# Layer 0's middle in a written order of TensorE, VectorE and ScalarE, and late modulation columns computed by TensorE

## Chip, cores and metric

The kernel runs on one core of one Trainium2 chip. Times are device microseconds (us) of one launch. Names: PE is TensorE, DVE VectorE, ACT ScalarE, POOL GpSimd, SP the engine that issues the DMAs spoken of here. The TensorE clock that the profile shows as granted is 1.00 at 2.4 GHz and 0.50 at 1.2 GHz; shares between are means over a stretch.

## What is computed

Two decoder layers on 1024 tokens of width 1024, in f32. Layer 0 has the even mixer, layer 1 the attention. The change concerns the even mixer and the modulation of both layers:

```python
def even_mixer(h, w_in, dw_w, dw_b, ln_w, ln_b, lam_re, lam_im, log_dt,
               b_re, b_im, c_re, c_im, d_skip, glu_w, glu_b, w_out):
    proj = h @ w_in
    a_in = proj[..., :2 * CONV_WIDTH]
    a_z = proj[..., 2 * CONV_WIDTH:3 * CONV_WIDTH]
    u = proj[..., 3 * CONV_WIDTH:3 * CONV_WIDTH + SSM_WIDTH]
    b_z = proj[..., 3 * CONV_WIDTH + SSM_WIDTH:]
    ya = conformer_conv(a_in, dw_w, dw_b, ln_w, ln_b) * jax.nn.silu(a_z)
    ys = jax.nn.gelu(s5_ssm(u, lam_re, lam_im, log_dt, b_re, b_im, c_re, c_im, d_skip), approximate=False)
    ys = ys * jax.nn.sigmoid(ys @ glu_w + glu_b)
    ys = ys * jax.nn.silu(b_z)
    return jnp.concatenate([ya, ys], axis=-1) @ w_out
```

`conformer_conv` is a gate, a causal depthwise convolution of 31 taps, a layer norm over channels and a SiLU; `s5_ssm` a diagonal complex recurrence. Each layer has 24 modulation columns of 128 numbers (8 shifts, 8 scales, 8 gates): the conditioning vector c times `mod_w`, plus `mod_b`.

## The kernel before

**Products.** Every large f32 product is done as three fp32r matmuls (`mm3`, L225 to L227): each operand is split into a rounded part and a rest (`split`, L203 on ScalarE and L206 on VectorE: `wh`, `wl` for weights, `h0h`, `h0l` for the hidden state). A projection of 128 output channels (`proj`) is two halves of 512 tokens (`pj`), each 8 blocks x 3 = 24 matmuls of 128x128 by 128x512. The GLU (`pg`) has 4 blocks, 12 matmuls a half; the output projection (`po`) comes last.

**State-space part.** `ssm_quarter(j)` does a quarter of the channels. Its head builds angles on VectorE (`T`, `TS`, L1387 to L1390) and sines on ScalarE (L1391 to L1393), powers on GpSimd (`HC`, L1402 to L1408), a small product `pk` on PE (L1417: eight matmuls of 128x32 by 128x128 in four column groups, by `tile_position`), a trip through DRAM (`Kd` to `M`, eight DMAs), and, with GpSimd's `G` and `GS` (L1438 to L1443), transposes `pgt`, products `sr`, `si`, the recurrence (`V`, `W`, scans L1469, `X`) and `py`. `TS`, `HT`, `G` and `GS` share a ring of three buffers (tag `t2`):

```python
n = L(f"TS{j}", "t2", [128, 4, 128], 3)
tt = L(f"HT{j}", "t2", sh, 3)
tg = L(f"GS{j}", "t2", sh, 3)
```

**Convolution.** `conv(j)` writes its gated input to DRAM and back (`Uc`), builds weight matrices `cm` on VectorE (L674), and multiplies (`pc`, L679, 64x64 tiles).

**Late modulation.** Sixteen columns of layer 0 are ready before the projections. The other 32 (8 gates of layer 0 and all of layer 1) come from `mod_cols`: two 256 KB DMAs a column (L253) into one buffer `mw` of two halves, two multiply-and-sum instructions on VectorE (L232) and an add (L255).

**Order.** A scheduler orders every engine's queue by priority: the program text gives the rank, and `prio` shifts it (`mod_cols` and the rope tables with 400000, which puts them behind other work that is ready by its reckoning). Each engine then runs its queue strictly in that order; a waiting instruction holds up all behind it on its engine.

Of the kernel before, what the change touches and what calls it, by code (L numbers as in the profile page):

```python
# [9 lines left out]
F32 = mybir.dt.float32  # L10
# [53 lines left out]

class Trunk:
# [30 lines left out]
    def prep(self):  # L96
# [22 lines left out]
        self.mod = [[self.consts.tile([128, 1], F32, name=f"mod{i}_{m}") for m in range(24)] for i in range(2)]  # L119
# [15 lines left out]
        self.g = [[self.consts.tile([128, 1], F32, name=f"g{i}_{m}") for m in range(8)] for i in range(2)]  # L135
# [99 lines left out]
    def mod_scale(self, layer, m):  # L235
        if 8 <= m < 16:
            nw = _cols()["norm_w"][0] + layer * 8 + m - 8
            self.nc.vector.scalar_tensor_tensor(self.g[layer][m - 8], self.mod[layer][m], 1.0, self.pk[:, nw:nw + 1],
                                                ALU.add, ALU.mult)

    def mod_bias(self, layer, m):
        o = _cols()["mod_b"][0] + layer * 24 + m
        return self.pk[:, o:o + 1]

    def mod_cols(self, cols):

        nc = self.nc
        w = self.u("mw", tag="mw")
        for layer, m in cols:
            h = self.c0.tile([128, 2], F32, tag="mh", name="mh", bufs=2)  # L250
            for i in range(2):
                c = slice(512 * i, 512 * i + 512)
                nc.sync.dma_start(w[:, c], self.I["mod_w"][layer, m][:, c])  # L253
                self.dot_c(h[:, i:i + 1], w[:, c], c)
            nc.vector.scalar_tensor_tensor(self.mod[layer][m], h[:, 0:1], h[:, 1:2], self.mod_bias(layer, m),  # L255
                                           ALU.add, ALU.add)
            self.mod_scale(layer, m)


    def layer0(self):  # L260
        nc, tc, I = self.nc, self.tc, self.I
        with self.cx0 as cx:
# [48 lines left out]
            with tc.tile_pool(name="start", bufs=8) as sp, order:  # L311
# [46 lines left out]
                def mods(m):  # L358
                    c = self.mod[0][m]
                    self.dot_c(c, mw[m], slice(0, 1024))  # L360
                    nc.vector.tensor_tensor(c, c, self.mod_bias(0, m), op=ALU.add)
                    self.mod_scale(0, m)
# [52 lines left out]
                pu, place = self.ssm_u_psum(ps, pm)  # L415
# [37 lines left out]
            self.ssm_params()  # L453

            def proj(j, evac):
                if j not in wt:
                    load_w(j, I["w0"][j], 8)
                hi, lo = wt.pop(j)
                for h in range(2):
                    p = ps(f"pj{j}_{h}")  # L460
                    s = slice(h * 512, (h + 1) * 512)
                    for k in range(8):
                        self.mm3(p, hi[:, k], lo[:, k], hh[k][:, s], hl[k][:, s], k == 0, k == 7)
                    evac(h, p)
# [4 lines left out]
            ysg = [None] * 4  # L469
            us = [self.ssm_u(j, pu) for j in range(3)]  # L470
            last = {}
            proj(15, lambda h, p: last.update({(3, h): p}))
            us.append(self.ssm_u(3, last))
            for j in range(4):
                self.ssm_quarter(j, us[j], pm, ysg)

            cut = lambda a, b: a.rearrange("p (t c) -> p t c", t=8)[:, :, b * 64:b * 64 + 64]
            late = lambda a: a.rearrange("p (c t) -> p t c", t=8)
            short = lambda a: a.rearrange("p (t c) -> p t c", t=8)
            acc = []  # L480
            for j in range(4):
                sg = [None, None]
                at = S(f"at{j}", tag="cv")

                def ev_gate(h, p):
                    sg[h] = E(f"sg{j}_{h}")
                    nc.scalar.activation(short(sg[h]), late(p), AF.Sigmoid)

                def ev_a(h, p):
                    nc.vector.tensor_tensor(cut(at, h), late(p), short(sg[h]), op=ALU.mult)  # L490

                proj(4 + j, ev_gate)
                proj(j, ev_a)
                acc.append(self.conv(j, at, pc))

            def ev_bz(h, p):
                t = E("z")
                nc.scalar.activation(short(t), late(p), AF.Silu)
                nc.sync.dma_start(self.bzd[j][:, h * 512:(h + 1) * 512], t)

            for j in range(4):
                proj(16 + j, ev_bz)

            with self.prio(400000):
                self.mod_cols([(0, m) for m in range(16, 24)] + [(1, m) for m in range(24)])
                self.rope_tables()


            sx.close()
            ga = cx.enter_context(tc.tile_pool(name="gluA", bufs=4))  # L510
            gx = cx.enter_context(ExitStack())
            gb = gx.enter_context(tc.tile_pool(name="gluB", bufs=4))
            zp = gx.enter_context(tc.tile_pool(name="z", bufs=4))
            Z = lambda: zp.tile([128, 512], F32, tag="z", name="z")
            ysh, ysl = [], []
            for j in range(4):
# [4 lines left out]
            for m in range(4):  # L521
                load_w(f"g{m}", I["glu_w"][m], 4)
                hi, lo = wt.pop(f"g{m}")
                for h in range(2):
                    p = ps(f"pg{m}_{h}")
                    s = slice(h * 512, (h + 1) * 512)
                    for k in range(4):
                        self.mm3(p, hi[:, k], lo[:, k], ysh[k][:, s], ysl[k][:, s], k == 0, k == 3)
                    t = E(f"gs{m}_{h}")
                    nc.scalar.activation(t, p, AF.Sigmoid, bias=self.P["glu_b"][:, m:m + 1])  # L530
                    nc.vector.tensor_tensor(ysg[m][:, s], ysg[m][:, s], t, op=ALU.mult)
# [10 lines left out]
            for j in range(4):  # L542
                for b in range(2):
                    yc[4 + j][b] = (gb, ga)[b].tile([128, 2, 512], F32R, tag="g", name=f"yc{4 + j}_{b}")
                    z = Z()
                    nc.sync.dma_start(z, self.bzd[j][:, b * 512:b * 512 + 512])
                    y = cut(ysg[j], b)
                    nc.vector.tensor_tensor(y, y, short(z), op=ALU.mult)
                    split_y(4 + j, ysg[j], b)


            for b in range(2):
                mu = pm(f"mu{b}")
# [1054 lines left out]
```

## Time and profile before

| | us |
|---|---|
| three runs: median (lowest to highest) | 1705.69 (1701.48 to 1708.97) |
| the profiled execution | 1709.29 |
| its span (first to last instruction) | 1707.5 |
| PE busy in it | 1654.8 (97%) |
| DVE busy | 1009.0 (59%) |
| ACT busy | 610.2 (36%) |
| POOL busy | 521.2 (31%) |
| layer 0's middle: first `pj` of layer 0 to first `pj` of layer 1 | 72.87 to 500.30 |

The profiled execution is 1.8 us longer than its span, and 3.6 us over the median of the runs. "Busy" counts the time in which an engine had an instruction running; for PE it counts the same at either clock.

### The profile page before, as it was taken

The numbers are of one execution on the slowest core, as the hardware profiler recorded it, in microseconds if no ns is written. First come the engines' busy times: TensorE is split into PE (matmuls) and PEld (weight loads), VectorE is DVE, ScalarE is ACT, GpSimd is POOL, SyncE is SP. The second block draws the span as 40 slices with busy tenths as digits, with TensorE's granted clock in tenths as the row PEclk, the third lists the DMA queues.
The fourth block names the chain that finished last, engine by engine and source line by source line (L and its number), as shares of the span: only waits on it lengthen the run. The fifth ranks groups of instructions, "written<-read, shape, count | busy, mean of one in ns | idle before, by whom it ended". The sixth has DMA issues, their size and how long they took to land.

```text
span 1707.5 us, 27738 instructions
## 1 busy us (share of the span) xinstructions
PE 1654.8 (97%) x9992; PEld 1516.7 (89%) x9992; DVE 1009.0 (59%) x2489; ACT 610.2 (36%) x1847; POOL 521.2 (31%) x737
## 2 busy tenths in 40 slices
PE   8989797999999999999999999999999999999999
PEld 5767576878789999999999999999999999999887
DVE  8987766175667545645754754754564575565541
ACT  5423231274534333333333334333333333343410
POOL 6466200100145323332431431432333233334000
PEclk9989898999999999999999999999999999999999
DMA  9366666313542112112212211211310211111252
GB/s 352 110 193 176 188 196 189 117 63 128 193 146 58 31 38 83 47 29 63 69 35 60 82 35 49 80 38 39 83 53 21 76 59 38 48 62 63 87 175 91
DMA packets 94186, 159.78 MB, mean 94 GB/s; under 512 B 13281, under 2 KB 43745, under 8 KB 94050
## 3 DMA queue, kind: packets, MB, share of 16 engines
q1 hardware_dynamic: 94050, 158.02, 30.2%
q8 instruction: 79, 1.29, 0.3%
q14 instruction: 57, 0.47, 0.1%
HBM read 130.54 MB, written 23.23 MB: 90 GB/s over the span
## 4 chain that ended last, share of the span: by engine, by line
PE 80%; DVE 1%; ACT 1%; POOL 0%; issue 0%; DMA 0%; DVEq 0%; ACTq 0%; POOLq 0%
PE pj L225 19%; PE pj L227 19%; PE pj L226 19%; PE O L985 4%; PE S L936 4%; PE po L227 3%; PE po L225 3%; PE po L226 3%; PE tqk L890 2%; PE tP L963 2%; DVE x L211 1%; PE pg L226 0%; PE pg L225 0%; PE pg L227 0%; PE pc L679 0%; DVE x L820 0%
## 5 line engine op out<-in xcount | busy, mean ns | idle before, releaser
L225 PE MATMUL pj<-wh,h 128*128 128x384 f32 x1536 | 544.0, 354 | 0.0
L227 PE MATMUL pj<-wh,h 128*128 128x384 f32 x1536 | 517.7, 337 | 0.8 <-DVE h L218 0.8
L226 PE MATMUL pj<-wl,h 128*128 128x384 f32 x1536 | 516.4, 336 | 0.0
L226 PEld LDWEIGHTS pj<-wl,h 128*128 128x128 f32 x1536 | 290.3, 189 | 0.3 <-issue 0.2
L225 PEld LDWEIGHTS pj<-wh,h 128*128 128x128 f32 x1536 | 289.6, 189 | 1.1 <-issue 0.2
L227 PEld LDWEIGHTS pj<-wh,h 128*128 128x128 f32 x1536 | 289.0, 188 | 1.4 <-DVE h L218 1.4
L875 POOL TENSOR_TENSOR B<-u,sin 128x256 f32<-128x256 f32 x192 | 190.3, 991 | 207.4 <-DVE u L871 207.4
L847 ACT ACTIVATE sq<-pj 128x128 f32<-128x128 f32 x384 | 103.0, 274 | 353.1 <-PE pj L227 327.5
L848 POOL TENSOR_SCALAR ss<-ss 128x2 f32<-128x2 f32 x192 | 41.2, 215 | 501.4 <-ACT sq L847 501.2
L206 DVE TENSOR_TENSOR wl<-raw,wh 128x768 fp32r<-128x768 f32 (+1 forms) x124 | 115.9, 949 | 123.9 <-ACT wh L203 123.3
L912 DVE COPY qk<-tqk 128x256 f32<-128x256 f32 x188 | 79.1, 421 | 139.6 <-PE tqk L890 139.6
L871 DVE SCALAR_TENSOR_TENSOR u<-pj,ss,pk 128x128 f32<-128x128 f32 x384 | 116.3, 344 | 75.7 <-POOL ss L849 75.7
L849 POOL TENSOR_TENSOR ss<-ss,mh 128x2 f32<-128x2 f32 x192 | 140.5, 732 | 16.0
L956 ACT ACTIVATE E<-E,nm 128x256 f32<-128x256 f32 (+2 forms) x128 | 71.3, 557 | 198.2 <-DVE nm L955 198.2
L226 PE MATMUL pj<-h0l,wh 128*128 128x512 f32 x272 | 110.2, 405 | 0.0
L227 PE MATMUL pj<-h0h,wl 128*128 128x512 f32 x272 | 109.1, 401 | 0.6 <-DVE wl L206 0.6
L225 PE MATMUL pj<-h0h,wh 128*128 128x512 f32 x272 | 109.6, 403 | 0.0
L883 DVE TENSOR_TENSOR u<-A,B 128x128 f32<-128x128 f32 x192 | 56.1, 292 | 88.0 <-POOL B L875 81.6
L203 ACT ACTIVATE wh<-raw 128x768 fp32r<-128x768 f32 (+1 forms) x124 | 97.5, 792 | 29.2 <-PE po L226 15.2
L882 DVE TENSOR_TENSOR A<-u,cos 128x256 f32<-128x256 f32 x192 | 96.6, 503 | 4.4
L936 PE MATMUL S<-qk 128*128 128x128 f32 x544 | 86.4, 274 | 0.0
L232 DVE CUSTOM_DVE_ANT_0 mw<-mw,cb 128x512 f32<-128x512 f32 (+1 forms) x72 | 61.5, 862 | 40.4 <-DMA mw<-in_mod_w 40.1
(429 smaller groups left out, 2858.1 us busy)
## 6 DMA issues: line engine op xcount, KB each, us to landing
raw<-in_wqkv SPq DMA_DIRECT2D x92, 384.0 KB
mw<-in_mod_w SPq DMA_DIRECT2D x64, 256.0 KB
wr<-in_w SPq DMA_DIRECT2D x17, 512.0 KB
al<-ad SPq DMA_DIRECT2D x16, 512.0 KB
wro<-in_wo SPq DMA_DIRECT2D x11, 512.0 KB
x<-in_x SPq DMA_DIRECT2D x8, 512.0 KB
mw<-in_mod_w SPq DMA_DIRECT2D x8, 512.0 KB
mw<-in_shift SPq DMA_DIRECT2D x8, 512.0 KB
```

The costliest lines, as they stand in the source:

```text
L203: nc.scalar.activation(hi, src, AF.Copy)
L206: getattr(nc, leng).tensor_tensor(lo, src, hi.bitcast(F32), op=ALU.subtract)
L225: mm(ps, lhsT=lh, rhs=rh, start=first, stop=False)
L226: mm(ps, lhsT=lh, rhs=rl, start=False, stop=False)
L227: mm(ps, lhsT=ll, rhs=rh, start=False, stop=last)
L847: sc.activation(sq[:, i], p[:, i * 128:(i + 1) * 128], AF.Square, accum_out=ss[:, i:i + 1])
L849: gp.tensor_tensor(ss, ss, mh, op=ALU.pow)
L871: v.scalar_tensor_tensor(u[:, i].rearrange("p a b -> p (a b)"), p[:, i * 128:(i + 1) * 128], ss[:, i:i + 1], w, ALU.mult, ALU.mult)
L875: gp.tensor_tensor(f(B), f(u), sin[:, ti].unsqueeze(1).to_broadcast([128, 4, 64]), op=ALU.mult)
L882: v.tensor_tensor(f(A), f(u), cos[:, ti].unsqueeze(1).to_broadcast([128, 4, 64]), op=ALU.mult)
L912: v.tensor_copy(out, tp)
L936: pe.matmul(ps[:, i * 128:(i + 1) * 128], lhsT=qT[h, g, t], rhs=kT[h, g, kt], start=True, stop=True)
```

## The change

From the first projection of layer 0 to the start of layer 1, the order of PE, DVE and ACT is that of the program text (`manual_schedule`); POOL and SP are ordered by the scheduler as before. The text is a loop over slots: 42 slots t of one half each (key 15, then 4, 0, 5, 1, 6, 2, 7, 3, then 16 to 19, g0 to g3, 8 to 11), then 21 slots of the output projection. A slot evacuates the half before it (`evac`), splits the next key's weights (`begin`), runs the side jobs that a table `side` gives for that slot, does a step of the modulation, and then issues its own 24 (or 12) matmuls. `ssm_quarter` and `conv` become generators that stop at each `yield`; step s of quarter j stands at slot 4j + (2, 3, 5, 6, 7, 7, 8, 11). The rope tables come at slot 1, layer norm at slots 25 to 34. PSUM: ring `ps` keeps 3 banks, `pm` goes from 3 to 2, and one bank `pr` is new.

`mod_cols` goes. `mod_rows` makes eight groups of four columns: in each of four steps two 256 KB DMAs bring weights with the input on partitions, and eight f32 matmuls (c repeated in 32 columns, by 128x128) run in four column groups; ACT copies the rows out, and `mod_turn` turns them into columns with one matmul `mc` of four columns and one add on DVE. The bytes fetched are the same.

```diff
-    def mod_cols(self, cols):
-        nc = self.nc
-        w = self.u("mw", tag="mw")
-        for layer, m in cols:
-            h = self.c0.tile([128, 2], F32, tag="mh", name="mh", bufs=2)
-            for i in range(2):
-                c = slice(512 * i, 512 * i + 512)
-                nc.sync.dma_start(w[:, c], self.I["mod_w"][layer, m][:, c])
-                self.dot_c(h[:, i:i + 1], w[:, c], c)
-            nc.vector.scalar_tensor_tensor(self.mod[layer][m], h[:, 0:1], h[:, 1:2], self.mod_bias(layer, m),
-                                           ALU.add, ALU.add)
...
+    def mod_rows(self, ps, pr):
...
+        w = self.u("mw", tag="mw").rearrange("p (i m n) -> p i m n", i=2, m=4)
+        crep = self.cb[:, 0:256].rearrange("p (k n) -> p k n", k=8)
+        rows = self.cb[:, 256:384]
+        p = pr("pr")[:, 0:128]
+        for n, (layer, m) in enumerate(MODR):
+            for q in range(4):
+                for i in range(2):
+                    nc.sync.dma_start(w[:, i], self.I["mod_r"][n, 2 * q + i])
+                yield
+                for i in range(2):
+                    k = 2 * q + i
+                    for j in range(4):
+                        nc.tensor.matmul(p[32 * j:32 * j + 32], lhsT=crep[:, k], rhs=w[:, i, j], start=(k == 0),
+                                         stop=(k == 7), tile_position=(0, 32 * j))
+            nc.scalar.activation(rows, p, AF.Copy)
+            self.mod_late = (ps, rows, layer, m)
...
+        c = ps(f"mc{layer}{m}")[:, 0:4]
+        nc.tensor.matmul(c, lhsT=rows, rhs=self.ident[:, 0::32], start=True, stop=True)
...
+            cx.enter_context(tc.manual_schedule(engines={mybir.EngineType.DVE, mybir.EngineType.Activation,
+                                                         mybir.EngineType.PE}))
...
+            seq = [15]
+            for j in range(4):
+                seq += [4 + j, j]
+            seq += [16, 17, 18, 19, "g0", "g1", "g2", "g3", 8, 9, 10, 11]
+            seq += [f"o{m}b" for m in range(5)] + [f"o{m}a" for m in range(5)]
+            seq += [f"o{m}" for m in range(5, 8)] + [f"p{m}" for m in range(8)]
...
+            def begin(i):
+
+                if i + 1 < len(seq) and seq[i + 1] not in wt:
+                    split_w(seq[i + 1])
...
+            at(1, self.rope_tables)
             for j in range(4):
...
+                for t in (2, 3, 5, 6, 7, 7, 8, 11):
+                    at(4 * j + t, next, quarter[j], None)
+                for t in (8, 9, 10, 12):
+                    at(4 * j + t, lambda j: next(conv[j], None), j)
...
+            for b in range(2):
+                at(25, ln_sum, b)
+                t = 27 + 4 * b
+                at(t, ln_mean, b)
+                at(t, ln_center, b, 0)
+                at(t + 1, ln_center, b, 1)
+                at(t + 2, ln_var, b)
+                at(t + 2, ln_rsqrt, b)
+                at(t + 3, ln_norm, b, (0, 1, 2, 3))
...
+            for t in range(42):
+                i, h = divmod(t, 2)
+                key = seq[i]
+                if done:
+                    evac(*done)
+                if h == 0:
+                    begin(i)
+                for fn in side.pop(t, ()):
+                    fn()
+                self.mod_turn()
+                if 4 <= t < 26 or t in (27, 31) or t > 33:
+                    mod_step()
+                p = ps(f"p{key}_{h}")
...
+                for k in range(n):
+                    self.mm3(p, hi[:, k], lo[:, k], rh[k][:, s], rl[k][:, s], k == 0, k == n - 1)
+                done = (key, h, p)
...
+            for k in range(8):
+                at(57 + k // 2, hidden, k)
...
         for t in range(8):
             nc.sync.dma_start(M[t::8], kd[:, :, (7 - t) * 16:(7 - t) * 16 + 128])
+        yield
```

**PE at the first quarter's `pk`.** Before, in the second projection (`pj_1_870` is its first key's second half, `pj_0_1486` the next key's first half, `pk_922` the quarter's product):

```order
L226 MATMUL pj_1_870<-h0l_753,wh_778 128x512
L227 MATMUL pj_1_870<-h0h_752,wl_779 128x512
L1417 MATMUL pk_922<-HC_909,bbd_820 32x128
L1447 MATMUL pgt_953<-ident,G_944 128x128 x4
L225 MATMUL pj_0_1486<-h0h_442,wh_782 128x512
L226 MATMUL pj_0_1486<-h0l_443,wh_782 128x512
L227 MATMUL pj_0_1486<-h0h_442,wl_783 128x512
L225 MATMUL pj_0_1486<-h0h_512,wh_782 128x512
L226 MATMUL pj_0_1486<-h0l_513,wh_782 128x512
L227 MATMUL pj_0_1486<-h0h_512,wl_783 128x512
L225 MATMUL pj_0_1486<-h0h_553,wh_782 128x512
L1417 MATMUL pk_922<-HC_909,bbd_820 32x128 x7
```

After (`p_1_857` is the half of slot 1, `p_0_936` that of slot 2):

```order
L232 MATMUL p_1_857<-h0l_714,wh_739 128x512
L233 MATMUL p_1_857<-h0h_713,wl_740 128x512
L1575 MATMUL pk_915<-HC_902,bbd_781 32x128 x8
L231 MATMUL p_0_936<-h0h_403,wh_743 128x512
L232 MATMUL p_0_936<-h0l_404,wh_743 128x512
L233 MATMUL p_0_936<-h0h_403,wl_744 128x512
```

One `pk` matmul, the transposes and seven large matmuls stood ahead of the other seven `pk`; now all eight stand ahead of slot 2's large matmuls.

**POOL for the same quarter, after the change** (the same six operations in the same order stand in the queue before it; `HC_902` is what `pk_915` reads, and `Activation` is ACT's semaphore):

```order
L1598 TENSOR_TENSOR GS_966<-bbi,pir 128x512 [waits DVE_49,Activation_49]
L1564 TENSOR_TENSOR HT_903<-pk,pr 128x512 [waits Pool_49]
L1599 TENSOR_TENSOR G_964<-G_964,GS_966 128x512 [waits Pool_49]
L1565 TENSOR_TENSOR HC_902<-HC_902,HT_903 128x512 [waits Pool_49]
L1601 TENSOR_TENSOR GS_966<-bbi,prr 128x512 [waits Pool_49]
L1566 TENSOR_SCALAR HC_902<-HC_902 128x512 [waits Pool_49]
```

What moved is not this queue but the angle `T` and its sines on DVE and ACT, whose buffer `TS` the first row takes over.

**DVE at the first angles.** Before (`T_901` is quarter 0, `T_1047` quarter 1; `h0l` belongs to the work ahead of the projections):

```order
L1387 TENSOR_TENSOR T_901<-pk,t_304 128x512
L1387 TENSOR_TENSOR T_1047<-pk,t_304 128x512
L218 SCALAR_TENSOR_TENSOR h0l_753<-x_332,mod_7_86,h0h_752 128x512
L1389 TENSOR_SCALAR TS_902<-T_901 128x512
L218 SCALAR_TENSOR_TENSOR h0l_753<-x_332,mod_7_86,h0h_752 128x512
L206 TENSOR_TENSOR wl_779<-wr_373,wh_778 128x1024
L1390 SCALAR_TENSOR_TENSOR TS_902<-TS_902,T_901 128x512
L206 TENSOR_TENSOR wl_783<-wr_375,wh_782 128x1024
```

After (`wl_889` is the split for key 0, in slot 2's `begin`; `ro` ends the rope tables of slot 1):

```order
L177 TENSOR_SCALAR ro<-ro 128x512
L182 SCALAR_TENSOR_TENSOR ro<-ro 128x512
L183 TENSOR_SCALAR ro<-ro 128x512
L212 TENSOR_TENSOR wl_889<-wr_338,wh_888 128x1024
L1545 TENSOR_TENSOR T_894<-pk,t_265 128x512
L1547 TENSOR_SCALAR TS_895<-T_894 128x512
L1548 SCALAR_TENSOR_TENSOR TS_895<-TS_895,T_894 128x512
L1579 COPY kp_779<-pk_915 128x128
```

Quarter 0's angle stood among the last hidden-state rests, quarter 1's beside it; now quarter 0's stands in slot 2 behind the split, and quarter 1's in slot 6.

**ACT in the layer norm's two halves.** Before (`lq` squares, `lr` the root, `cv` the SiLU of the normed convolution, `z` the gate of a projection):

```order
L186 ACT_TABLE_LOAD
L186 ACTIVATE lr_3102<-va_3085,eps 128x512
L188 ACTIVATE lr0t<-lr_3102 128x512
L564 ACTIVATE lq_3126<-cv_1697 128x512
L567 ACTIVATE lq_3129<-cv_1920 128x512
L579 ACT_TABLE_LOAD
L579 ACTIVATE z<-pj_0_3225 128x512
L564 ACTIVATE lq_3134<-cv_2143 128x512
L567 ACTIVATE lq_3137<-cv_2366 128x512
L574 ACTIVATE cv_1697<-cv_1697,pk 128x8x64
```

After (`gs` is the GLU's sigmoid, `whg` its weights):

```order
L683 ACTIVATE gs_0_2970<-pg_0_2957,pk 128x512
L192 ACT_TABLE_LOAD
L192 ACTIVATE lr_2976<-va_2973,eps 128x512
L194 ACTIVATE lr0t<-lr_2976 128x512
L683 ACT_TABLE_LOAD
L683 ACTIVATE gs_1_2997<-pg_1_2984,pk 128x512
L209 ACTIVATE whg_3000<-wrg_2791 128x512
L607 ACT_TABLE_LOAD
L607 ACTIVATE cv_1532<-cv_1532,pk 128x8x64
L607 ACTIVATE cv_1946<-cv_1946,pk 128x8x64
L607 ACTIVATE cv_2361<-cv_2361,pk 128x8x64
L607 ACTIVATE cv_2700<-cv_2700,pk 128x8x64
```

The layer norm stood among the projections 8 to 11, whose gates are SiLU too; now it stands among the GLU halves, with a table load at each change of function.

## Rows read from the trace of the kernel before

**Rows 1.** Busy time by engine over layer 0's middle, with PE's granted clock.

```profile
core 0: us, PE busy (x) PEld busy (x) DVE busy (x) ACT busy (x) POOL busy (x), PEclk, DMA share, GB/s
72.87:500.30 427.43, 389.03 (x2368) 309.06 (x2366) 280.21 (x480) 155.75 (x227) 108.26 (x81) 0.93 0.53 164
```

**Rows 2.** PE's waits in that stretch, by what ended them (total, times, longest).

```profile
PE pc L679 <- DVE cm L674: 8.3, 3, 4.6
PE py L1491 <- DVE X L1479: 7.3, 3, 4.0
PE pc L679 <- DMA Uc<-Cd: 5.8, 2, 3.5
PE py L1487 <- DMA mw<-in_mod_w: 5.8, 1, 5.8
PE po L227 <- DVE wlo L206: 5.2, 1, 5.2
```

**Rows 3.** Timeline of PE: start, duration; 44 matmuls between the two rows' starts.

```profile
319.67 0.39 PE L226 MATMUL pj<-h0l,wh 128*128 128x512 f32 x1
...
329.94 0.39 PE L225 MATMUL pj<-h0h,wh 128*128 128x512 f32 x1
```

**Rows 4.** Timeline of PE around one wait.

```profile
202.91 1.50 PE L679 MATMUL pc<-Uc,cm 64*64 64x126 f32 x42
210.19 1.19 PE L1487 MATMUL py<-U,M 128*128 128x128 f32 x4 [5.77 <-DMA mw<-in_mod_w]
```

**Rows 5.** Two-microsecond stretches behind that wait; columns as in rows 1.

```profile
214.00:216.00 2.00, 2.00 (x5) 1.09 (x4) 2.00 (x4) 0.00 (x0) 0.00 (x0) 0.51 0.40 131
216.00:218.00 2.00, 2.00 (x44) 1.72 (x44) 2.00 (x7) 0.00 (x0) 0.00 (x0) 1.00 0.30 90
```

**Rows 6.** DVE's group of late modulation: busy, mean ns, idle before it.

```profile
L232 DVE CUSTOM_DVE_ANT_0 mw<-mw,cb 128x512 f32<-128x512 f32 x64 | 51.0, 804 | 38.5 <-DMA mw<-in_mod_w 38.2
```

**Rows 7.** Timeline of PE around quarter 1's `pk` (two records a call).

```profile
107.78 0.68 PE L1487 MATMUL py<-U,M 128*128 128x128 f32 x4
108.40 0.67 PE L1417 MATMUL pk<-HC,bbd 128*32 128x128 f32 x16
108.99 0.50 PE L225 MATMUL pj<-h0h,wh 128*128 128x512 f32 x1
109.33 0.39 PE L226 MATMUL pj<-h0l,wh 128*128 128x512 f32 x1
```

**Rows 8.** Groups of ACT in the middle, as in rows 6.

```profile
L203 ACT ACTIVATE wh<-wr 128x1024 fp32r<-128x1024 f32 x15 | 15.8, 1056 | 48.9 <-PE pj L226 42.0 <-PE pj L227 5.1 <-PE pg L226 1.8
...
L487 ACT ACT_TABLE_LOAD x6 | 7.7, 1283 | 3.6 <-PE pj L227 3.5
L574 ACT ACTIVATE cv<-cv,pk 128x512 f32<-128x512 f32 x8 | 5.8, 806 | 0.0
...
L1391 ACT ACTIVATE T<-TS 128x512 f32<-128x512 f32 x4 | 2.5, 631 | 32.0 <-DVE TS L1390 32.0
```

**Rows 9.** Groups of DVE in the middle, as in rows 6.

```profile
L206 DVE TENSOR_TENSOR wl<-wr,wh 128x1024 fp32r<-128x1024 f32 x17 | 25.3, 1491 | 6.2 <-ACT wh L203 6.2
L1469 DVE TENSOR_TENSOR_SCAN W<-m,V 128x128 f32<-128x128 f32 x32 | 16.2, 569 | 0.0
...
L1390 DVE SCALAR_TENSOR_TENSOR TS<-TS,T 128x512 f32<-128x512 f32 x4 | 3.9, 981 | 0.0
...
L1387 DVE TENSOR_TENSOR T<-pk,t 128x512 f32<-128x512 f32 x2 | 1.4, 676 | 0.0
...
L1389 DVE TENSOR_SCALAR TS<-T 128x512 f32<-128x512 f32 x3 | 1.2, 412 | 0.0
```

**Rows 10.** Timeline of POOL in quarter 0's head: first and last of six operations.

```profile
78.41 1.82 POOL L1439 TENSOR_TENSOR GS<-bbi,pir 128x512 f32<-128x512 f32 x1 [1.43 <-ACT T L1392]
...
86.54 1.51 POOL L1408 TENSOR_SCALAR HC<-HC 128x512 f32<-128x512 f32 x1
```

**Rows 11.** Timeline of PE where it meets them.

```profile
88.11 0.66 PE L1417 MATMUL pk<-HC,bbd 128*32 128x128 f32 x14 [0.48 <-POOL HC L1408]
```

More of the change, by code (lines that the diff above doesn't have):

```diff
@@ L453, in layer0 @@
             self.ssm_params()
[L455 to L464, printed above, removed]
+            nc.vector.tensor_copy(self.cb[:, 0:256].rearrange("p (k n) -> p k n", k=8),
+                                  self.ccol.unsqueeze(2).to_broadcast([128, 8, 32]))
@@ L467, in layer0 @@
             sx = cx.enter_context(ExitStack())
             self.sp = sx.enter_context(tc.tile_pool(name="ssm", bufs=1))
[L469 to L477, printed above, removed]
+            ysg, acc, us = [None] * 4, [None] * 4, [None] * 4
@@ L478, in layer0 @@
+            for j in range(3):
+                us[j] = self.ssm_u(j, pu)
+            cutb = lambda a, b: a.rearrange("p (t c) -> p t c", t=8)[:, :, b * 64:b * 64 + 64]
             late = lambda a: a.rearrange("p (c t) -> p t c", t=8)
             short = lambda a: a.rearrange("p (t c) -> p t c", t=8)
-            acc = []
-            for j in range(4):
[L482 to L510, printed above, removed]
@@ L520, in layer0 @@
                 ysl.append(b)
[L521 to L531, printed above, removed]
+            at(21, glu_pools)
@@ new lines, in layer0, with ln_sum, ln_mean @@
+            for j, t in enumerate((21, 22, 23, 24)):
+                at(t, split_s, j)
+            ln = [{}, {}]
+            def ln_sum(b):
+                q = ln[b]["q"] = wp.tile([128, 512], F32, tag="cm", name=f"ls{b}")
+                for j in range(1, 4):
+                    nc.gpsimd.tensor_tensor(short(q), cutb(acc[j], b), short(q) if j > 1 else cutb(acc[0], b), op=ALU.add)
+            def ln_mean(b):
+                ln[b]["mu"] = pm(f"mu{b}")
+                nc.tensor.matmul(ln[b]["mu"], lhsT=self.ones, rhs=ln[b]["q"], start=True, stop=True)
@@ new lines, in ln_center, with ln_var @@
+            def ln_center(b, i):
+                mu = ln[b]["mu"]
+                q = []
+                for j in (2 * i, 2 * i + 1):
+                    x = cutb(acc[j], b)
+                    nc.vector.scalar_tensor_tensor(x, short(mu), -2.0, x, ALU.mult, ALU.add)
+                    q.append(E(f"lq{b}{j}"))
+                    nc.scalar.activation(short(q[-1]), x, AF.Square)
+                nc.vector.tensor_tensor(q[1], q[1], q[0], op=ALU.add)
+                ln[b][i] = q[1]
+            def ln_var(b):
+                ln[b]["va"] = pm(f"va{b}")
+                for i in range(2):
+                    nc.tensor.matmul(ln[b]["va"], lhsT=self.ones, rhs=ln[b][i], start=(i == 0), stop=(i == 1))
@@ L577, in ev_az, with load_z @@
[L577 to L587 removed]
+            zs = {}
+            def load_z(j, b):
+                zs[j, b] = Z()
+                nc.sync.dma_start(zs[j, b], self.bzd[j][:, b * 512:b * 512 + 512])
@@ L590, in layer0 @@
+            evac(*done)
+            mod_step()
             self.h1 = [[None, None] for _ in range(8)]
             self.x1 = [None] * 4
-            def out_mm(p, m, b, hi, lo, ks, first, last):
-                for i, k in enumerate(ks):
-                    self.mm3(p, hi[:, i], lo[:, i], yc[k][b][:, 0], yc[k][b][:, 1], first and i == 0,
-                             last and i == len(ks) - 1)
-            def residual(p, m, b, xr):
-                x, out = self.x1, self.out if self.stop0 else self.x1d
+            xr = {}
@@ L647, in first_slabs @@
+            residual(*done)
+            assert not side, side.keys()
     def first_slabs(self):
```

310 lines of the change are left out of this document (203 added, 107 removed).

## The prediction

> **What bounds the kernel now.** I read the table of busy times first: PE is busy 97% of the span, so only what PE waits for, and the clock it runs at, can change the time. The change touches layer 0's middle alone, so I cut that stretch out, from 72.87 to 500.30 us: 427.4 us, of which PE is busy 389.0, at a mean granted clock of 0.93 [rows 1]. The reader should take two amounts from that row. The first is idle time: 427.4 - 389.0 = 38.4 us. The second is clock: (1 - 0.93) x 427.4 = 30 us of work not done at full speed. About 2 us of that fell into the waits themselves, so I take 28 us, with 26 to 30 as bounds.
>
> The two amounts hang together. The waits by releaser [rows 2] are few and long: ten of them make 32.4 of the 38.4 us. PE waits for `cm` and `X` of VectorE, for `Uc`, for a transfer, and once for `wlo`. Behind one such wait, which ends at 210.19 [rows 4], the clock is at 0.51 in the stretch up to 216 and at 1.00 in the next [rows 5]: 5.8 us at the 1.2 GHz level, so 2.9 us lost on top of a wait of 5.8. Over all, 28 us for ten long waits is 2.8 us each. I price a restart at 3 us, with 2.3 (28 us over twelve waits) and 5 as bounds.
>
> The matmuls of a projection are 10.27 / 44 = 0.2334 us apart at full clock [rows 3]. A slot of 24 is thus 5.6 us of PE, a slot of 12 is 2.8 us. The order of these matmuls cannot change that.
>
> Where the waits come from is seen on VectorE. The 64 multiply-and-sum instructions of the modulation take 51.0 us and idle 38.2 us for their transfers [rows 6]. `cm` and `X` stand in VectorE's queue behind them. Removing them is a real cure for most of the 38.4 us.
>
> **What the change takes away, at most.** If all waits of the middle and all low clock went, 38.4 + 28 = 66.4 us would be won: 1709.3 - 66.4 = 1642.9 us. The rest of the sum is what comes back.
>
> **New matmuls.** 32 steps of eight f32 matmuls in four column groups. The nearest row is `pk`: the same shapes, columns in four groups, eight calls from 108.40 to 108.99, that is 0.59 us; and the large matmul behind it takes 109.33 - 108.99 = 0.34 us to the next, 0.11 more than 0.2334 [rows 7]. So 32 x (0.59 + 0.11) = 22.4 us. The eight little `mc` come on top: at most as much as a `py` call in the same rows, 0.62 / 2 = 0.31, so 1.6 us at about 0.2 each. Together 24 us, bounds 19 (no switching) and 26. It all lies on PE's path.
>
> The Trainium skill, page "TensorEngine Tiling (Array Packing)", section "Key Properties", says that different tiles can run their matmuls in parallel and that changing the tiling mode drains TensorE. The first agrees with the 0.59 us. The second speaks against the change: 64 mode changes; with 0.11 us for each, going in and coming out, its cost would be 7 us and the sum 3.5 us higher. No row shows the way in by itself.
>
> **The four `pk` waits.** This is the largest term. In the rows of PE's order, all eight `pk` now stand ahead of slot 2's 24 matmuls (and so in slots 6, 10 and 14), and PE cannot go round them. `pk` reads `HC`; POOL's queue has `GS` ahead of the last `HC` operations, and `GS` takes over `TS`, which ScalarE must have read. In the trace before, `GS` started at 78.41, released by ScalarE's `T`, and the last of the six operations that end `HC` started at 86.54 and ended at 88.05 [rows 10]: 9.64 us, 1.6 us each. PE met them at 88.11 with a wait of only 0.48 us [rows 11], because the angles had been made early and large matmuls filled the time. Now `T` stands on VectorE in the same slot, behind the slot's split of weights, and the split behind ScalarE's `wh`, which follows the end of the slot before on PE. From the moment when PE arrives, the chain is, for slot 2: a copy `ut` on ScalarE 0.6 (as a 128x512 `T`), `wh` 1.06 [rows 8], `wl` 1.49, `T` and `TS` 0.68 + 0.41 + 0.98 [rows 9], two sines or magnitudes 2 x 0.62 [rows 8], POOL 9.64: 16.1 us, in which PE has nothing else. Slot 6: no `ut`, but four scans of 0.57 [rows 9] ahead of `T`: 17.8 us. Slots 10 and 14: POOL's order there has only four operations from `GS` to the end of `HC`, 6.4 us, so 14.5 us; ahead of `pk` PE has 80 records of the convolution, at 1.50 us for 42 [rows 4] 2.9 us, so 11.7 us each. Sum 16.1 + 17.8 + 2 x 11.7 = 57.3 us. Bounds: 45, if POOL's twenty operations take 1.0 us each, as VectorE's slowest of the same size does (0.98), and 65, if the rope tables, which stand ahead of slot 2 on VectorE and ScalarE, end late and GpSimd's copies add to slot 6. Queued behind the wait on PE are the slot's own matmuls, and with them everything the other engines evacuate later; none of it can run ahead.
>
> **Layer norm among the GLU halves.** PE needs 2.8 us for a GLU half, 11.2 for four. ScalarE's written list between the two norms (the rows of its order) has in these four halves four table loads of 1.28 and four SiLU of 0.81 [rows 8], nine more operations on 128x512 at about 0.63, a root of 0.7 and a `wh` of 1.06: 16 us, and some 3 us of waiting for VectorE and `va`. Against PE's 11.2 us and 1.2 of `mu` and modulation that leaves 6.5 us of waiting for `va` in slot 33, and about 2.5 us in slot 29, where the list starts late: 9 us, bounds 7 and 12. Before, these loads lay under 24-matmul halves and cost nothing.
>
> **The rest.** In the output projection the wait for `wlo`, 5.2 us [rows 2], arises because VectorE has the residuals, the splits and the hidden state of layer 1 in a few slots; the same work is now spread over four slots of 5.6 us. I take 5 us again, bounds 0 and 9. Late transfers of modulation weights: 5.8 us once in the waits before [rows 2]; the next weights have a whole slot to come, unless SP is busy with `M` or `Yd`: 2 us, bounds 0 and 7. The removed VectorE instructions themselves are worth nothing beyond the 38.4 us already taken off, since PE covers VectorE elsewhere.
>
> **Restarts.** Four `pk` waits, one for `va`, and half a one for the rest: 5.5 x 3 = 16.5 us (bounds 12 and 26).
>
> **Sum.** 1642.9 + 24 + 57.3 + 9 + 5 + 2 + 16.5 = 1756.7 us against the profiled execution. That one was 3.6 us over the median of the runs, so 1753 us beside 1705.7. With all low bounds: 1709.3 - 38.4 - 30 + 19 + 45 + 7 + 0 + 0 + 12 - 3.6 = 1720; with all high bounds: 1709.3 - 38.4 - 26 + 26 + 65 + 12 + 9 + 7 + 26 - 3.6 = 1786.
>
> **Rivals.** (a) *Faster: the `pk` waits do not arise.* If VectorE and ScalarE reach `T` early enough, POOL is done with `HC` when PE arrives. Then the four waits and their restarts, 57.3 + 12 = 69.3 us, fall out: 1684 us. For it speaks that POOL is little used (31%) and that the trace shows PE meeting `HC` with 0.48 us to wait. Against it: the order puts `T` behind `wl`, and `wl` behind ScalarE's work on the half that PE has just ended. It decides below 1753 - 1705.7 = 47 us less, that is, if the four waits with restarts come to under 22 us, 5.5 each in place of 17. Chance 0.05.
>
> (b) *The GLU part costs more.* If every table load ends as a wait of PE, eight loads and the sigmoid behind each, 8 x 1.9 = 15 us, come on top: 1768 us. For: the loads stand in a strict order between halves of 2.8 us. Against: some lie beside matmuls. Chance 0.12.
>
> (c) *The column groups run one after another in this use, or their transfers come late.* At 0.31 us a call [rows 7] 256 calls are 79 us in place of 22: 1810 us. For: each set reads other weights than the one before, where `pk` repeats small ones. Against: the shapes are those of `pk`. Chance 0.05.
>
> (d) *The change does less than its waits:* POOL takes its short times everywhere and the restarts cost 2.3 us, the other terms as above: 1753 - 12 - 4 = 1737 us. Chance 0.10.
>
> **How the numbers follow.** My forecast has 0.68, rivals b and d lie within its bounds. The predicted time is 1753 us. Rival a (0.05) and c (0.05) lie outside; some of the forecast's own case does too. The range is 1720 to 1786 us, about 0.8. What a measurement of this kernel can tell from no change is about 0.5%, 1697 to 1714 us. Faster than that: rival a, 0.05. Within it: rival d and the forecast with two more terms at nothing, 0.04. Slower: 0.91.
>
> **What would show it.** Right: PE waiting 10 to 18 us for POOL's `HC` at four places 30 to 45 us apart, from about 85 us on, each followed by some microseconds at 0.50; PE waiting for `va` twice; no wait for `cm` or `X` worth naming; 32 groups of `pr` matmuls of 0.6 to 0.7 us. The middle would be some 47 us longer than 427. Wrong: `pk` waits under 6 us each, or `pr` groups above 1 us, or PE waiting most for something not named here, such as `G` for the transposes or the evacuation of a PSUM bank, since `pm` has one bank less.

## The result

The changed kernel takes 1765.7 us (median of four runs, 1763.2 to 1767.7) against 1705.5 us of the kernel before beside it: a ratio of 1.0353, 95% interval 1.0325 to 1.0381, so 60 us or 3.5% slower. The prediction was 1753 us, range 1720 to 1786.

All of it lies in layer 0's middle, from the first large matmul of layer 0 (72.38 us) to the first of layer 1 (560.40 us): 488.0 us, where it was 427.4 [rows 1]. The rest of the span is 1205.3 us now and was 1207.2. Two stretches of the changed kernel, columns as in [rows 1]:

```profile
72.38:560.40 488.02, 409.36 (x2896) 316.02 (x2895) 209.55 (x323) 164.87 (x242) 96.13 (x83) 0.92 0.46 143
560.40:1765.70 1205.30, 1199.37 (x7331) 1158.08 (x7329) 666.59 (x1851) 421.37 (x1566) 373.30 (x579) 1.00 0.21 61
```

PE is idle for 488.0 - 409.4 = 78.7 us of it, where it was 38.4, and busy for 409.4, where it was 389.0. I also cut both stretches into pieces of 1 us and summed PE's busy time times the granted clock, which gives its work at full speed: 390.2 us now and 366.2 before, so 24.0 us of new matmuls. What busy time lost to the lower clock is the rest, 19 us now and 23 before. PE's waits by releaser in that stretch (total, times, longest), to be read against [rows 2]:

```profile
PE pk L1575 <- POOL HC L1566: 47.1, 4, 15.1
PE pr L266 <- DMA mw<-in_mod_r: 11.0, 8, 3.2
PE pop L231 <- ACT whp L209: 10.2, 2, 9.4
PE va L598 <- DVE lq L592: 6.0, 3, 3.6
PE mc L279 <- ACT cb L268: 1.4, 2, 1.0
PE pop L233 <- DVE wlp L212: 1.3, 3, 0.5
PE poo3b L231 <- ACT who3a L209: 1.0, 1, 1.0
PE poo L233 <- DVE wlo L212: 0.5, 1, 0.5
```

The reader should see both halves of the change in these two lists. The waits for `cm`, `X` and `Uc`, which led [rows 2], are gone, and of the 5.2 us for `wlo` 0.5 are left. In their place stands `pk`, which waits for GpSimd's `HC` four times, 47.1 us; before, it met `HC` with 0.48 us to wait [rows 11].

The first of the four, in PE's timeline (start, duration, idle before it), answers to [rows 11], and GpSimd's six operations to [rows 10]:

```profile
99.17 1.10 PE L1575 MATMUL pk<-HC,bbd 128*32 128x128 f32 x14 [15.08 <-POOL HC L1566]
```

```profile
73.33 1.61 POOL L1561 TENSOR_TENSOR HT<-pk,pi 128x512 f32<-128x512 f32 x1
74.90 1.55 POOL L1597 TENSOR_TENSOR G<-bbr,prr 128x512 f32<-128x512 f32 x1
76.41 1.47 POOL L1562 TENSOR_TENSOR HC<-HC,HT 128x512 f32<-128x512 f32 x1
91.58 1.31 POOL L1598 TENSOR_TENSOR GS<-bbi,pir 128x512 f32<-128x512 f32 x1 [13.70 <-ACT T L1550]
...
97.62 1.50 POOL L1566 TENSOR_SCALAR HC<-HC 128x512 f32<-128x512 f32 x1
```

GpSimd stands still from 77.9 to 91.58 us, released at last by ScalarE's `T` (13.70 us), and from there its six operations take until 99.12 us, all of which PE spends waiting, since 84.1. The clock behind the four waits, which end at 99.17, 142.31, 195.49 and 250.35 us, in stretches of two microseconds (for the second and third only the stretch in which it rises):

```profile
99.00:101.00 2.00, 1.83 (x16) 1.33 (x17) 0.53 (x2) 0.00 (x0) 1.92 (x5) 0.50 0.00 0
101.00:103.00 2.00, 2.00 (x6) 1.52 (x6) 0.00 (x0) 0.00 (x0) 1.66 (x3) 0.50 0.18 61
103.00:105.00 2.00, 2.00 (x8) 1.62 (x7) 0.00 (x0) 0.00 (x0) 0.00 (x0) 0.72 0.27 55
148.00:150.00 2.00, 2.00 (x9) 1.60 (x9) 1.95 (x4) 0.00 (x0) 0.00 (x0) 0.88 0.00 0
198.00:200.00 2.00, 2.00 (x7) 1.58 (x6) 2.00 (x6) 0.00 (x0) 1.79 (x6) 0.58 0.89 214
250.00:252.00 2.00, 1.65 (x30) 1.49 (x30) 0.44 (x2) 0.00 (x0) 2.00 (x3) 0.50 0.67 236
252.00:254.00 2.00, 2.00 (x10) 1.48 (x5) 2.00 (x3) 0.00 (x0) 1.92 (x2) 0.50 0.50 124
254.00:256.00 2.00, 2.00 (x9) 1.59 (x9) 2.00 (x5) 0.00 (x0) 0.31 (x1) 0.93 0.64 200
```

It is at the 1.2 GHz level when PE starts again, and back at 2.4 GHz 4.9, 6.2, 4.2 and 3.9 us later: 9.6 us lost on top of the four waits.

### The profile page after: what moved, and what is told of

It is laid out like the page before. It is cut to its first block, busy times and chain, and to the rows that moved or that the text cites. A ratio compares the mean times of both kernels' runs of the same rounds, so it can differ in the third digit from the quotient of the medians.

```text
span 1765.7 us, 28609 instructions
## 1 busy us (share of the span) xinstructions
PE 1675.6 (95%) x10520; PEld 1524.2 (86%) x10520; DVE 937.0 (53%) x2332; ACT 618.7 (35%) x1860; POOL 505.3 (29%) x737
## 4 chain that ended last, share of the span: by engine, by line
PE 84%; issue 5%; DVE 3%; POOL 3%; ACT 2%; DMA 1%; SPq 0%; POOLq 0%; ACTq 0%; DVEq 0%
PE pj L233 17%; PE pj L231 17%; PE pj L232 17%; PE O L1142 4%; PE S L1093 4%; PE p L231 4%; PE p L232 3%; PE p L233 3%; PE tqk L1047 2%; PE tP L1120 2%; PE po L233 2%; PE po L231 2%; PE po L232 2%; PE pr L266 1%; DMA mw<-in_mod_r 1%
## 5 line engine op out<-in xcount | busy, mean ns | idle before, releaser
L231 PE MATMUL p<-h0h,wh 128*128 128x512 f32 x272 | 114.8, 422 | 0.0
L232 PE MATMUL p<-h0l,wh 128*128 128x512 f32 x272 | 110.6, 407 | 0.0
L233 PE MATMUL p<-h0h,wl 128*128 128x512 f32 x272 | 110.0, 404 | 0.0
L1093 PEld LDWEIGHTS S<-qk 128*128 128x128 f32 x544 | 80.9, 190 | 1.3
```

The costliest lines, as they stand in the source:

```text
L231: mm(ps, lhsT=lh, rhs=rh, start=first, stop=False)
L232: mm(ps, lhsT=lh, rhs=rl, start=False, stop=False)
L233: mm(ps, lhsT=ll, rhs=rh, start=False, stop=last)
L1093: pe.matmul(ps[:, i * 128:(i + 1) * 128], lhsT=qT[h, g, t], rhs=kT[h, g, kt], start=True, stop=True)
```

## The experiments

Every kernel is compared with the kernel before in runs on the same chip. "The middle" is the stretch from the first large matmul of layer 0 to the first of layer 1, in the profiled execution. That execution lies within 4 us of the median of its kernel, but for e6, where it took 1725.3 us, the longest of six: its middle and its waits are those of a long execution.

| run | what it changes in the changed kernel | time, us | ratio to before (95%) | the middle, us |
|---|---|---|---|---|
| changed kernel | | 1765.7 | 1.0353 (1.0325 to 1.0381) | 488.0 |
| e1 | angles two slots early | 1725.9 | 1.0108 (1.0089 to 1.0128) | 447.9 |
| e2 | `TS` in a buffer of its own | 1724.3 | 1.0098 (1.0083 to 1.0113) | 447.2 |
| e4 | no late modulation | 1725.5 | 1.0104 (1.0087 to 1.0121) | 448.6 |
| e5 | modulation steps off three slots | 1757.1 | 1.0296 (1.0283 to 1.0310) | 478.0 |
| e3 | slabs in the last slot | 1762.0 | 1.0319 (1.0303 to 1.0336) | 475.1 |
| e8 | slabs through another ring | 1764.5 | 1.0328 (1.0313 to 1.0343) | 486.2 |
| e12 | the same, split in the last slot | 1757.3 | 1.0304 (1.0289 to 1.0319) | 477.1 |
| e7 | SiLU for the GLU's sigmoid | 1764.6 | 1.0341 (1.0328 to 1.0354) | 484.4 |
| e6 | e1, e5 and e8 together | 1717.6 | 1.0067 (1.0049 to 1.0085) | 445.1 |
| e9 | e6, rope tables at slot 3, modulation from slot 6 | 1713.7 | 1.0040 (1.0028 to 1.0052) | 432.6 |
| e10 | e2, e12, rope tables and modulation as in e9 | 1705.6 | 0.9996 (0.9987 to 1.0005) | 423.2 |
| e11 | e10, modulation's transfers first | 1697.3 | 0.9948 (0.9934 to 0.9962) | 418.4 |

**Is it the angles that hold up `pk`, and by what path?** Two edits take away the same wait in different places. The first makes the angles two slots earlier:

```diff
-                for t in (2, 3, 5, 6, 7, 7, 8, 11):
+                for t in (0, 2, 3, 5, 6, 7, 7, 8, 11):
...
         nc.scalar.activation(y, y, AF.Sin, scale=-TURN, bias=self.quarter)
+        yield
```

> The angles T of each quarter, with their sines, are made two slots earlier (a yield behind them, slot 4j instead of 4j+2); all else as in the changed kernel. My theory (GpSimd's GS waits for TS, and the end of HC stands behind GS): the four pk waits, 47.1 us in the changed kernel, fall under 5 us, and with them about 10 us lost at half clock behind them; time about 1710 us, 1700 to 1718. Rival 1 (GpSimd's own work bounds pk, whatever the angles do): pk still waits 30 us or more, time 1750 or more. Rival 2 (the time goes into the next wait, for the transposes or for the modulation's transfers): pk waits gone, time still above 1730.

The second leaves the angles where they are and only takes `TS` out of the ring that `GS` uses:

```diff
...
-        n = L(f"TS{j}", "t2", [128, 4, 128], 3)
+        n = L(f"TS{j}", "ts", [128, 4, 128], 1)
```

> The angles stay in their slots, but TS gets a buffer of its own, so that GS no longer takes over TS (32 bytes for it come from packing eight scale columns into one tile). My theory: it is the shared ring, not the place of the angles, that holds up HC; pk waits under 5 us and about 1710 us, as when the angles are moved. Rival (HC is late because GpSimd starts it late, or the sines themselves are awaited by pk): pk waits stay above 30 us and the time above 1750.

Waits of PE in the two, first with the early angles, then with the buffer:

```profile
PE pr L266 <- DMA mw<-in_mod_r: 14.8, 14, 2.0
...
PE pgt L1607 <- DVE kp L1580: 6.5, 1, 6.5
...
PE pk L1576 <- POOL HC L1567: 0.4, 1, 0.4
```

```profile
PE pr L267 <- DMA mw<-in_mod_r: 13.7, 14, 2.1
...
PE pgt L1607 <- DVE kp L1580: 4.8, 1, 4.8
PE pk L1576 <- POOL HC L1567: 3.6, 1, 3.6
```

47.1 us of waiting become 0.4 and 3.6. GpSimd's own work does not bound `pk`, and the sines are not what `pk` awaits: with a buffer of its own `TS` can be as late as before. So the path is the shared ring. The times, 1726 and 1724 us, lie 16 and 14 us above what I expected, and the second rival of e1 holds that much: a wait for the transposes `pgt` (6.5 and 4.8 us) and more of the waits for modulation weights (14.8 and 13.7 in place of 11.0) take back some of the 57 us that the waits and the clock behind them should have given. Of the clock, 5 to 6 us came back in place of 10: the sum over 1 us pieces that gave 19 us lost gives 14 and 13 here.

**What does the late modulation cost?** e4 leaves out its transfers, `pr` and `mc`; the columns are the biases.

```diff
+            for layer, m in MODR:
+                t = self.consts.tile([128, 4], F32, name=f"mod{layer}_{m}")
+                nc.vector.tensor_copy(t, self.mod_bias(layer, m, 4))
...
-                if 4 <= t < 26 or t in (27, 31) or t > 33:
-                    mod_step()
...
```

> The late modulation is left out: no transfers of its weights, no pr and mc matmuls; the late columns are the biases alone. My theory: it costs its matmuls (32 steps of 0.65 with 0.11 of switching, 24 us), the 11 us of waits for its transfers and some 3 us of clock: about 1728 us, 1722 to 1735. Rival 1 (the matmuls fill time in which PE would have waited anyway, for HC above all): 1745 or more. Rival 2 (its 16.8 MB also hold up other transfers): below 1718.

The middle becomes 39.4 us shorter, of which 10.5 are idle time of PE and 28.9 busy time. The price of one undisturbed step stands in the changed kernel's timeline:

```profile
121.78 0.64 PE L266 MATMUL pr<-mw,cb 128*32 128x128 f32 x16
122.35 0.50 PE L231 MATMUL p<-h0h,wh 128*128 128x512 f32 x1
122.69 0.40 PE L232 MATMUL p<-h0l,wh 128*128 128x512 f32 x1
```

From 121.78 to 122.35 are 0.57 us for eight matmuls, and the large matmul behind them takes 0.34 us to the next, as behind `pk` in [rows 7]. The column groups do run side by side. 32 such steps are 22 us; eight `mc` at 0.3 are 2.5. The remaining 4 of the 28.9 us are clock: the sum over 1 us pieces gives 19.1 us lost in the changed kernel and 14.5 in e4. The step at 230.60, for one, starts at half speed behind a wait of 3.20 us and takes 1.28.

**Where do the waits for its weights come from?** e5 moves the steps off slots 9, 13 and 17, in which SP issues `M` and `Yd`.

```diff
-                if 4 <= t < 26 or t in (27, 31) or t > 33:
+                if 2 <= t < 28 and t not in (9, 13, 17) or t == 31 or t > 33:
```

> The changed kernel with the modulation's steps taken out of slots 9, 13 and 17 and put into slots 2, 3, 26 and thereabouts instead; same number of steps. Theory: PE's 11 us of waits for the modulation's weights arise because SP issues the sixteen small transfers of M and Yd in those slots ahead of the next weights; the waits fall under 4 us, time about 1757 us, 1753 to 1760. Rival: with one buffer the weights are late in any slot whose SP queue is busy, the waits only move; 8 us or more of them remain and the time is 1763 or more.

The waits fall from 11.0 to 4.0 us and the time to 1757 us, as expected:

```profile
PE pr L266 <- DMA mw<-in_mod_r: 4.0, 4, 1.7
```

SP's queue in the changed kernel around 226 us (start, duration, issues) shows the two transfers behind the eight of `Yd`; they were wanted at 227.4:

```profile
222.02 3.87 SPq L1660 DMA_DIRECT2D Yd<-Y  x8
225.99 2.59 SPq L261 DMA_DIRECT2D mw<-in_mod_r  x2
```

The repair holds only beside the `pk` waits. In e9 and e10, with most of the `pk` waits repaired and the steps off the same slots, 9.6 and 10.3 us of waits for these weights are back at other steps. The queue behind `M` and `Yd` is thus not their only cause; a second buffer for the weights was not tried.

**What makes the wait for `whp`?** In the output projection PE has one wait of 9.37 us, which ends at 538.12. I had put such a wait down to VectorE's work on layer 1's hidden state. The trace of the changed kernel offered another cause: the first slabs of layer 1 (`fr`), opened in slot 58.

```diff
-            at(58, open_slabs)
+            at(62, open_slabs)
```

> The four first weight slabs of layer 1 are opened in the last slot instead of slot 58. Theory A, from the trace of the changed kernel: the 9.4 us wait for whp comes from SP's queue, where the residual's xr stands behind a slab that waits for a buffer; the wait goes, with some 4 us of half clock behind it: about 1752 us, unless layer 1 then starts later for want of its slabs (up to 5 us back). Theory B, that of my prediction: VectorE's work on the hidden state of layer 1 in four slots makes the wait; then it stays above 5 us and the time within 4 us of the changed kernel's 1765.

> The changed kernel with the first slabs of layer 1 loaded through the large ring of twenty buffers in place of the ring of five that the residual's xr uses; they stay in slot 58. Theory: the slab that waits for a buffer ahead of xr on SP was the cause of the 9.4 us wait for whp; it falls under 2 us, layer 1's slabs are not late, and the time is about 1752 us, 1749 to 1756, better than with the slabs in the last slot. Rival: xr itself waits for a buffer of its ring, so the wait stays above 5 us and the time above 1760.

The last slot for the slabs takes 12.9 us from the middle, with VectorE's work unchanged, but layer 1 then starts without its slabs: what follows the middle takes 1210.3 us in place of 1205.3, and the time is 1762 us, where I had expected 1752. The other ring alone leaves 5.4 of the 9.4 us, and the time hardly moves: 1764.5, where I had expected 1752 again. ScalarE's timeline of the changed kernel shows the part that was left out of that expectation: the slabs' splits stand in its written order, one waits 4.46 us for its transfer, and `whp` stands behind them:

```profile
527.40 2.30 ACT L209 ACTIVATE wh<-fr 128x768 fp32r<-128x768 f32 x3
534.16 0.84 ACT L209 ACTIVATE wh<-fr 128x768 fp32r<-128x768 f32 x1 [4.46 <-DMA fr<-in_wqkv]
536.50 0.63 ACT L732 ACTIVATE xq<-x 128x512 f32<-128x512 f32 x1 [1.49 <-DVE x L726]
537.03 1.04 ACT L209 ACTIVATE whp<-wrp 128x1024 fp32r<-128x1024 f32 x1
```

So e12 loads them in slot 58, through the large ring, and splits them in slot 62:

```diff
             at(58, open_slabs)
+            at(62, self.split_slabs)
```

> The slabs of layer 1 are loaded in slot 58 through the large ring, but ScalarE and GpSimd split them in the last slot only. Theory: two things made the 9.4 us wait for whp, SP's queue (which the ring alone took away, 3 us of the 9) and ScalarE's written list, where the splits of slabs that are still on their way stand ahead of whp. With both gone the wait is under 2 us, layer 1 finds its slabs, and the time is about 1752 us, 1748 to 1756. Rival (the 1.5 MB of slabs on the DMA engines make xr late wherever they are split): waits in that place of 5 us or more, 1760 or more.

The longest wait for `whp` is 1.4 us, the middle is 10.9 us shorter than in the changed kernel, and the time 1757 us, 5 more than expected: small waits for `wlp` (2.9 us) and for `st` (1.2) in the last slots remain.

**Do table loads set the layer norm's wait?** e7 puts a SiLU in the place of the GLU's sigmoid.

> The changed kernel with a SiLU in place of the GLU's sigmoid, so that ScalarE needs no table load between the GLU's gates and the SiLU of the convolution branch; this changes the GLU's gate. My prediction's reason (ScalarE's list of eight table loads and their neighbours is longer than PE's GLU halves): four loads go, the three waits for va, 6.0 us in the changed kernel, fall under 3 us, time 1759 to 1764. Rival (VectorE's centring and adds set va): the waits stay at 5 us or more and the time does not move.

Of the three waits for `va` (1.2, 1.2 and 3.6 us) one of 1.2 goes, 4.8 us stay, and the time does not move, as the rival said. The reason given in the prediction is wrong for the largest. In the changed kernel, the wait that ends at 391.48 us has ScalarE idle twice for VectorE's `cv`, and VectorE's `cv` stands behind the next key's split `wl` (start 387.55):

```profile
386.64 0.69 DVE L684 TENSOR_TENSOR yt<-yt,gs 128x512 f32<-128x512 f32 x1
387.55 1.23 DVE L212 TENSOR_TENSOR wl<-wr,wh 128x1024 fp32r<-128x1024 f32 x1 [0.23 <-ACT wh L209]
388.69 1.28 DVE L589 SCALAR_TENSOR_TENSOR cv<-mu,cv 128x512 f32<-128x512 f32 x2
390.73 0.69 DVE L592 TENSOR_TENSOR lq<-lq,lq 128x512 f32<-128x512 f32 x1 [0.76 <-ACT lq L591]
```

That the split makes the wait was read from these rows and not tried.

**Do the repairs add up, and is there a version that beats both kernels?**

> Angles two slots early, modulation steps off the three slots, slabs through the other ring, together. If the three losses add: 1726 less 9 for the steps less 13 for the slabs, 1704 us, 1699 to 1709, within 0.5% of the kernel before. Rival (they overlap, one wait takes the place of another): 1715 or more.

> As the three repairs, and the rope tables at the end of slot 3's side jobs instead of slot 1, the modulation starting at slot 6 (it shares the buffer). Theory: with the angles early, the 6.5 us wait for the transposes comes from the rope tables on VectorE, stretched beside GpSimd, ahead of the copy kp; it goes with its restart: some 8 us under the three repairs, about 1696 us, 1690 to 1701, faster than the kernel before. Rival: the rope tables hold up what follows slot 3 on VectorE (at, the products V and W) as much as they held up kp: no gain over the three repairs, 1703 or more.

> All repairs that held, with the written order kept: TS in its own buffer, rope tables at slot 3, modulation from slot 6 and off slots 9, 13 and 17, slabs split in the last slot. If the angles no longer matter to GpSimd, the 7.5 us wait for HC that came with the rope tables goes too: 1714 less 7.5 and 3 of clock, less 8 to 12 in the output projection: about 1694 us, 1688 to 1700, faster than the kernel before by 0.4 to 1%. Rival (a new wait takes the place, for the products behind the angles or for the modulation's weights): 1705 or more.

> As all repairs, with the modulation's transfers ahead of the rest of M and Yd in SP's queue. Theory: the waits for the modulation's weights (some 9 us with the repairs) fall under 3 us without any for M in their place: 6 to 9 us under all repairs. Rival: M, and py with it, comes late by as much, because a transfer that waits for its buffer holds up SP: no gain or a loss.

The first three miss what I expected. The first gives 1717.6 us for 1704: the slabs' part was worth nothing in that form (1 us alone, above), and the rest adds up within 2 us. Moving the rope tables, and with them the modulation's first steps, gives 1713.7 us for 1696, another 4 us: the 6.5 us wait for `pgt` goes, but a wait of 7.5 us for `HC` comes in slot 6, since quarter 1's angle now stands behind the rope tables. With `TS` in its own buffer (e10, 1705.6 us for 1694) that wait is GpSimd's for 0.8 us only, and yet not gone. Waits of PE in e10, then in e11:

```profile
PE pr L267 <- DMA mw<-in_mod_r: 10.3, 9, 2.3
PE pk L1582 <- DVE V L1631: 5.9, 1, 5.9
PE pop L234 <- DVE wlp L213: 2.9, 4, 1.3
PE va L599 <- DVE lq L593: 2.4, 2, 2.1
...
PE pk L1582 <- POOL HC L1573: 0.8, 1, 0.8
```

```profile
PE pr L268 <- DMA mw<-in_mod_r: 8.0, 12, 1.7
PE pk L1583 <- DVE V L1632: 5.9, 1, 5.9
PE va L600 <- DVE lq L594: 2.4, 1, 2.4
```

`pk` now waits 5.9 us for VectorE's `V`, which reads the PSUM banks of `sr` and `si`: `V` stands behind the rope tables on VectorE, and the ring `pm`, from which `pk` takes its bank, has two banks where it had three; a third was not tried, so that this is the cause is read from the order and not shown. e10 is level with the kernel before. e11 puts the modulation's transfers ahead in SP's queue:

```diff
...
-                for i in range(2):
-                    nc.sync.dma_start(w[:, i], self.I["mod_r"][n, 2 * q + i])
+                with self.prio(-50000):
+                    for i in range(2):
+                        nc.sync.dma_start(w[:, i], self.I["mod_r"][n, 2 * q + i])
```

It takes another 8 us, the amount expected, but not by the way expected: the waits for the weights were to fall under 3 us and fall from 10.3 to 8.0. In the profiled executions the middle is 4.8 us shorter and starts 1.1 us earlier; where the rest of the 8 us comes from is open. At 1697.3 us it is 0.52% (0.38 to 0.66) faster than the kernel before, in a written order too, though with the rope tables, the modulation's steps and the slabs' splits in other slots than in the changed kernel.

## Why the prediction was right, and where its sizes were off

**What the change takes away.** Right in the main: the waits for `cm`, `X` and `Uc` vanished, and e10 and e11 show that what was left, 24 us of matmuls included, fits into the time before once most of the new waits are repaired. The clock was taken too high. I put 2 of the 30 us at low clock into the waits themselves; by the sum over 1 us pieces 6 lay there, and 23, not 28, could be won back.

**The four `pk` waits.** Right in place and cause, and e1 and e2 show the path through the ring. The size was 57.3 us, measured 47.1: 15.1, 13.8, 9.1 and 9.1 for 16.1, 17.8, 11.7 and 11.7. I had taken GpSimd's 1.6 us an operation from a stretch in which VectorE worked beside it; with VectorE still, the six took 7.54 us, 1.26 each, and the twenty of all four waits 25.5 in place of 32.1. In slots 6, 10 and 14 the chain ahead of them was shorter too, by 1.4 to 2.0 us. So two of the waits missed the 10 to 18 us that I had named as the sign, and they came 44, 58 and 55 us apart, not 30 to 45.

**Restarts.** 12 us forecast behind `pk`, 9.6 measured. Behind the longest wait for `va` 6.2 us at half speed are 3.1, as forecast.

**Modulation.** The matmul's price was right: 0.57 and 0.11 us, for 0.59 and 0.11 forecast, and 24.0 us more work at full speed in all, for 24; nothing is left for a price of the way into the column groups. The step that was mis-sized is the late transfers, "2 us, bounds 0 and 7": they cost 11.0 us of waiting, outside the bounds, because in the largest waits a step's two transfers are issued only when the one buffer is free, and then behind up to sixteen others on SP; some 4 us of half clock come with them, and 1.4 us of waits for `mc`, which I had left out. The term as a whole was 26 us and measured 39.

**Layer norm.** 9 us forecast, 6.0 measured, in three waits and not two, and the reason, table loads, holds for one wait of 1.2 us only.

**The output projection.** 5 us forecast, 13.0 measured (`whp` 10.2, `wlp` 1.3, `who3a` 1.0, `wlo` 0.5), and for another cause: transfers and splits of layer 1's slabs in the written order of ScalarE, shown by e3, e8 and e12. VectorE's work there, which the prediction named, is not it. Half a restart was allowed for; behind this wait some 6 us at half speed are 3 us.

**The sum.** In the middle of the profiled executions 474.8 us were forecast (427.4 and 47.4 more) and 488.0 measured, 13 more. Too much stood for `pk`, 10 us, and for the layer norm, 3. Too little stood for what follows: 5 us for the clock, which could not be won back, 10 for the modulation's waits, 8 for the output projection, and some 3 for all restarts (19.1 for 16.5). That is 26 against 13, and leaves nothing large unexplained. That the time came so near to 1753 is thus partly luck: half of what was too low was made up for by what was too high. Outside the middle the span became 2 us shorter, which I had not forecast.

**The rivals.** The trace excludes a, and e7 excludes b. Of c, the column groups one after another are excluded by the 0.57 us; that the transfers come late was true, at 11 us of waiting and not 57. The two parts of d were each partly true, GpSimd at 1.26 us an operation and restarts of 2.4 us, but the other terms came out larger.

## What to carry to other kernels

When an order is written by hand for some engines and left to a scheduler on others, follow each wait across the border: here GpSimd's queue had the same order as before, but one of its operations, `GS`, took over a buffer whose last reader had been moved into the written part, and PE's whole queue stood behind it. A ring shared by tiles of different stages is a dependency that no data flow shows; a buffer of 2 KB a partition was worth 41 us. Before moving work into a written order, look for waits on transfers among what it puts into the queue: every one of them holds all that stands behind it.

## What the hardware showed that I had not expected

VectorE's simple operations took much longer while GpSimd ran. The rope tables' operation at L173 took 0.43 us with GpSimd still and 1.22 us beside it, in the same kernel and shape, and GpSimd's gap is that of the rows above (77.9 to 91.58):

```profile
74.00 1.22 DVE L173 TENSOR_SCALAR ro<-ro 128x512 f32<-128x512 f32 x1
75.26 1.48 DVE L174 TENSOR_SCALAR ro<-ro 128x512 f32<-128x512 f32 x1
76.77 3.12 DVE L176 SCALAR_TENSOR_TENSOR ro<-ro 128x512 f32<-128x512 f32 x3
79.92 0.43 DVE L173 TENSOR_SCALAR ro<-ro 128x512 f32<-128x512 f32 x1
80.38 0.43 DVE L174 TENSOR_SCALAR ro<-ro 128x512 f32<-128x512 f32 x1
80.84 2.14 DVE L176 SCALAR_TENSOR_TENSOR ro<-ro 128x512 f32<-128x512 f32 x3
```

The Trainium skill, page "SBUF — State Buffer", section "SBUF: two separate sides", says that certain VectorE operations and those of GpSimd share a pair of ports as an exclusive lock: whichever starts first holds it for its whole instruction, and the other blocks. These rows agree in kind: 1.22 and 1.48 us in place of 0.43, about as long as the GpSimd operations of 1.61, 1.55 and 1.47 us that ran beside them. It would also explain, which no run tried, why the `pk` waits came out shorter than I had worked out, and why in e1, where GpSimd had no gap, the rope tables on VectorE took 15.7 us in place of 11.4.
